# Parked scores fetched up to four blocks ahead, into the slots of the normed rows

## The chip, the cores and the metric

One core of one Trainium2 chip runs the whole program in one launch. The metric is the time of an execution on the device in microseconds, the median of several executions. SP below is SyncE, whose queue issues most of the DMAs.

## The reference

Two layers of a streaming encoder, for 512 prompt tokens (one new stream) and 128 sample tokens (8 running streams of 16), width 1024. Layer 0 mixes tokens by a gated convolution beside windowed attention, layer 1 by a gated linear recurrence (HGRN2). Each mixer is followed by PEER, a retrieval from 16,384 experts: product keys choose for every token and each of 8 heads the best 16 of them, and the output sums over the experts found

```python
for each token x, each head, each of its 16 experts e (index idx, gate g):
    y += g * gelu(dot(x, u[e])) * v[e]
```

Everything is float32; on TensorE a product of float32 is made of three products of high and low halves.

## The kernel before, in words

**Two ways through PEER.** The 128 sample tokens and the first 128 prompt tokens go the sparse way: POOL gathers the rows of u (line 880) and of v (line 913) by index, VectorE makes the dot products (line 884) and the weighted sums `yv` (line 920). The other 384 prompt tokens go the dense way, in `dense_peer`: all 16,384 experts in 128 blocks of 128. A block's scores are a product of the 384 normed rows `xhl` with 128 rows of u, and Gelu; they are multiplied by the gates of the block (`gch`, one table for four blocks, fetched at lines 1105 and 1107; the multiply is line 1110), split into halves `wt` (high on ScalarE, line 240, low on VectorE, line 241), and combined with the block's 512 KB of v (line 272, also split into `whi` and `wlo`) in 18 matmuls of 128 x 512, line 1122, that gather in six banks over all 128 blocks.

**Scores made ahead.** While the product keys are being chosen, TensorE has room. `ahead` makes the scores of the last blocks then and parks them in DRAM, `sd`, 192 KB a block: the last 72 of layer 0 (blocks 56 to 127), the last 94 of layer 1 (blocks 34 to 127). In the main loop `scores(k)` fetches such a block at line 1096; for the blocks before, it makes the product.

**Slots.** A name of a tile pool ("tag") has a fixed number of buffers; a tile takes the next, and the instruction that first writes it waits for the last use of the tile that had it. Fetched scores lie in "ge" (two slots); in layer 1, where `DEEP` is 126, in "ge" and "sq" by turns (four in all); in layer 0 `DEEP` is 54, so that the fetched blocks, 56 and up, have "ge" alone. A slot is free when the low half of the block that was in it has been taken (line 241). "xb" has four slots of 128 x 2 x 512. In the loop they hold four of the eight tiles of the normed rows `xhl`, which the last product reads (block 55 in layer 0, block 33 in layer 1). They have a second user in layer 0's loop: the sample tokens, which were done with PEER before, go on into layer 1's mixer while the prompt's loop runs. The sample's recurrence works in two units, and each unit takes two tiles of "xb" (`lins` in `hgrn`), one held until its outputs are made (`recur`, lines 669 to 715), the other until its states are (`states`, lines 717 to 735).

**Order.** Loop, sparse rows and recurrence are generators stepped by turns, and a list scheduler then orders each engine's instructions. In the loop `scores` runs one to two blocks ahead of `combine`. Each engine executes its instructions in this order, and a DMA issue that waits holds up SP's issues behind it.

Of the kernel before, what the change touches and what calls it, by code (L numbers as in the profile page):

```python
# [62 lines left out]
def kernel(ctx: ExitStack, tc: tile.TileContext, t: dict):  # L63
    nc = tc.nc
    V, S, P, T, Y = nc.vector, nc.scalar, nc.gpsimd, nc.tensor, nc.sync
# [10 lines left out]
    def tl(tag, shape, dt=F32, name=None):  # L76
        return sb.tile(shape, dt, name=name or tag, tag=tag, bufs=BUFS.get(tag, 1))
# [4 lines left out]
    def bank(tag):  # L82
        return ps.tile([128, 512], F32, name="p" + tag, tag=tag, bufs=1)
# [100 lines left out]
    def behind(ins, others):  # L184
        for d in others:
            tc.add_manual_dep(ins.ins, d.ins.name, mybir.DependencyInfo(
                mybir.DependencyClass.Sync, mybir.DependencyReason.DATA), reason="gates in DRAM")
# [33 lines left out]
    def small(tag, n, name=None):  # L221
        return tl(tag, [128, 512 if n > 128 or tag != "idf" else 128], name=name)[:, :n]
# [16 lines left out]
    def split(hi, lo, src):  # L239
        S.activation(hi, src, AF.Copy)  # L240
        return V.tensor_tensor(lo, src, hi.bitcast(F32), op=OP.subtract)  # L241
# [27 lines left out]
    def halves(tags, shape, src):  # L269

        raw = tl(tags[0], shape, name="wraw")
        Y.dma_start(raw, src)
        hi = tl(tags[1], shape, F32R, name="whi")
        lo = tl(tags[2], shape, F32R, name="wlo")
        d = split(hi, lo, raw)
        if tags[0] == "u4":
            mark[0] = d
        marks.append(d)
        return hi, lo

    def product2(p, w, xhl, first=None):
        for xv, wv in ((0, 0), (1, 0), (0, 1)):
            for k in range(8):
                m = T.matmul(p, w[wv][:, k], xhl(xv, k), start=(k == 0 and xv == wv), stop=(k == 7 and wv == 1))
                if first is not None:
                    follow(m, first)
                    first = None

    def product(p, w, xhl):
        for k in range(8):  # L290
            T.matmul(p, w[0][:, k], xhl(0, k), start=(k == 0), stop=False)  # L291
            T.matmul(p, w[0][:, k], xhl(1, k), start=False, stop=False)  # L292
            T.matmul(p, w[1][:, k], xhl(0, k), start=False, stop=(k == 7))  # L293
# [680 lines left out]
    def dense_peer(l, xhl, sv, si):  # L974

        G = GA
        n = G.n
        FIRST, EACH, NA = FE[l]
        AHEAD = list(range(128 - NA, 128))
        nt = len(G.tiles)  # L980
        gd = dr.tile([n // 32, 128, 128, 32], F32, name="gd", tag="gd", bufs=1)
        sd = dr.tile([len(AHEAD), 128, n], F32, name="sd", tag="sd", bufs=1)
# [106 lines left out]
        gch = {}  # L1089
        mult = [None, None]  # L1090

        def scores(k):
            deep = DEEP[l] > k
            ge = small(("ge", "sq")[k % 2] if deep else "ge", n)
            if k in AHEAD:
                Y.dma_start(ge, sd[AHEAD.index(k)])  # L1096
            else:
                w = halves(("u4", "uh", "lo"), [128, 8, 128], t["uT"][l, k])
                s = bank("b" if k < KB[l] and k % 2 else "s")[:, :n]
                product2(s, w, xhl, mult[1] if PEO[l] else None) if PO[l] else product(s, w, xhl)  # L1100
                S.activation(ge, s, AF.Gelu)
            if k % 4 == 0:
                gch[k // 4] = tl("g8", [128, n // 32, 4, 32], name="gch")
                if SC[l]:
                    behind(Y.dma_start(gch[k // 4][:, 0:4], gz[:, :, k:k + 4, :].rearrange("g p k t -> p g k t")), fences[-1:])
                g0 = 4 * SC[l]
                Y.dma_start(gch[k // 4][:, g0:], gd[g0:, :, k:k + 4, :].rearrange("g p k t -> p g k t"))
            g3 = ge.rearrange("p (g t) -> p g t", t=32)
            marks.append(None)
            marks[-1] = mult[0] = V.tensor_tensor(g3, g3, gch[k // 4][:, :, k % 4], op=OP.mult)  # L1110
            wt = tl(("w3", "nat")[k % 2] if deep else "w3", [128, 2, 384], F32R, name="wt")[:, :, :n]
            marks.append(split(wt[:, 0], wt[:, 1], ge))
            return wt
# [13 lines left out]
        for k in range(128):  # L1127
            while len(wts) <= (2 if DEEP[l] > k + 2 else 1):
                j = next(todo, None)
                if j is None:  # L1130
                    break
                wts[j] = scores(j)
                if DEEP[l] <= j + 1 and j not in vhs:
                    vhs[j] = values(j)
            for j in (k, k + 1):
                if j < 128 and j not in vhs:
                    vhs[j] = values(j)
            combine(k, wts.pop(k), vhs[k])
            mark[0] = mult[0]
            yield 1  # L1140
# [69 lines left out]
    for l in range(2):  # L1210
# [31 lines left out]
        xa = lambda v, k, xhl=xhl: xhl(v, k)[:, 128:512]  # L1242
        xt = lambda v, k, xhl=xhl: xhl(v, k)[:, 0:128]
        de = dense_peer(l, xa, sv[:, 1:4], si[:, 1:4])
        for i, _ in enumerate(route_p(l, xhl, sv, si)):
            if i < FE[l][0]:
# [124 lines left out]
```

## Time and profile before

| what | us |
|---|---|
| median of the runs | 4003.3 |
| range of the runs | 4000.8 to 4003.57 |
| the profiled execution's own time | 4001.81 |
| its span | 4000.1 |
| layer 0's loop, fetched blocks: from, to the last combine | about 1555, 2095.1 |
| of these, last weighted sum of layer 0's gathered rows | 1850.0 |
| sample's indices of layer 1 done (line 874) | 2162.0 |
| layer 1's mixer ends (line 339) | 2616.6 |
| layer 1's loop, fetched blocks: from, to the last combine | about 3540, 3969 |

Every time is of one core, and one profiled execution; the page divides the span into busy time by engine, slices, queues, the chain that ended last and groups of instructions. A group's busy time is not its cost: what counts is which engine the others wait for in that stretch. PE is TensorE, DVE VectorE, ACT ScalarE, POOL GpSimd; SPq is SP's queue of DMA issues.

### The profile page before, as it was taken

The page shows a single profiled execution, that of the slowest core. Times are in us where ns is not written, and L with a number is a line of the kernel's source. Part 1 is how long each engine was busy: PE and PEld are TensorE (multiplying, and loading weights), DVE is VectorE, ACT ScalarE, POOL GpSimd, SP SyncE. Part 2 cuts the span into 40 slices and gives each one's busy share as a digit, 9 for nine tenths or more (in the row PEclk, how much of TensorE's full clock was granted, in tenths as well). Part 3 has the DMA queues.
Part 4 walks back from the last instruction along what each step waited for, and adds up shares of the span by engine and source line. Part 5 has one row for each costly group of instructions (what it writes and reads, how often), then busy time and mean ns, then how long its engine had stood idle before and what let it go on. Part 6 is the DMA issues. An engine that isn't in the chain of part 4 may idle for free. (4 is left out here: it accounts for less than half of the span.)

```text
span 4000.1 us, 51433 instructions
## 1 busy us (share of the span) xinstructions
PE 3573.7 (89%) x17676; PEld 2922.7 (73%) x17676; DVE 3217.6 (80%) x6206; ACT 1654.5 (41%) x2717; POOL 1606.3 (40%) x1173
## 2 busy tenths in 40 slices
PE   6978788999999999788998777887999999999997
PEld 4756666789779998556776555566998988987775
DVE  5558999886568779988669877999998638888988
ACT  6544222467623334344434223331367733333332
POOL 0001665431235455541002544465078734454444
PEclk8989899999999999999999787798999999999998
DMA  4334998896689999999766775688467769999999
GB/s 143 118 105 155 333 341 312 314 344 246 248 301 338 338 340 349 376 347 316 238 204 227 268 237 201 214 319 309 138 170 200 200 202 349 339 361 388 385 385 328
DMA packets 491783, 1102.40 MB, mean 276 GB/s; under 512 B 55920, under 2 KB 271984, under 8 KB 486384
## 3 DMA queue, kind: packets, MB, share of 16 engines
q1 hardware_dynamic: 325632, 562.10, 40.4%
q0 software_dynamic: 165888, 537.01, 37.9%
q8 instruction: 139, 2.28, 0.2%
q14 instruction: 124, 1.02, 0.1%
HBM read 1008.28 MB, written 91.59 MB: 275 GB/s over the span
## 5 line engine op out<-in xcount | busy, mean ns | idle before, releaser
L240 ACT ACTIVATE whi<-wraw 128x1024 fp32r<-128x1024 f32 x710 | 741.5, 1054 | 1115.8 <-PE py L292 336.1
L241 DVE TENSOR_TENSOR wlo<-wraw,whi 128x1024 fp32r<-128x1024 f32 x710 | 861.6, 1216 | 339.5 <-ACT whi L240 174.3
L880 POOL DMA_INDIRECT gu<-u,idx x512 | 675.4, 1319 | 1059.2 <-DVE idx L874 425.6
L1122 PE MATMUL py<-whi,wt 128*128 128x512 f32 x3072 | 798.4, 405 | 53.7 <-ACT wt L240 48.0
L1122 PEld LDWEIGHTS py<-whi,wt 128*128 128x128 f32 x3072 | 581.7, 192 | 209.4 <-ACT wt L240 66.0
L913 POOL DMA_INDIRECT gv<-v,idx x384 | 510.0, 1328 | 530.7 <-DVE yv L920 355.7
L884 DVE CUSTOM_DVE_ANT_0 gu<-gu,xnn 128x1024 f32<-128x1024 f32 x512 | 614.8, 1217 | 59.0 <-DMA gu<-u,idx 58.4
L291 PE MATMUL py<-xhl,whi 128*128 128x512 f32 (+1 forms) x1392 | 540.2, 389 | 72.5 <-ACT xhl L240 30.5
L293 PE MATMUL py<-xhl,wlo 128*128 128x512 f32 (+1 forms) x1392 | 534.8, 385 | 24.5 <-DVE wlo L241 24.3
L292 PE MATMUL py<-xhl,whi 128*128 128x512 f32 (+1 forms) x1392 | 531.0, 381 | 10.7 <-DVE xhl L241 10.7
L920 DVE SCALAR_TENSOR_TENSOR yv<-gv,wact,yv 128x1024 f32<-128x1024 f32 x381 | 488.3, 1282 | 5.2 <-DMA gv<-v,idx 2.1
L291 PE MATMUL ps<-xhl,whi 128*128 128x384 f32 (+1 forms) x1168 | 403.4, 345 | 20.0 <-ACT whi L240 9.9
L293 PE MATMUL ps<-xhl,wlo 128*128 128x384 f32 (+1 forms) x1168 | 403.2, 345 | 6.0 <-DVE wlo L241 5.9
L1122 PE MATMUL py<-wlo,wt 128*128 128x512 f32 x1536 | 400.5, 393 | 0.7 <-DVE wlo L241 0.7
L292 PE MATMUL ps<-xhl,whi 128*128 128x384 f32 (+1 forms) x1168 | 399.8, 342 | 0.0
L291 PEld LDWEIGHTS py<-xhl,whi 128*128 128x128 f32 x1392 | 274.6, 197 | 131.6 <-ACT xhl L240 34.9
L1122 PEld LDWEIGHTS py<-wlo,wt 128*128 128x128 f32 x1536 | 288.0, 188 | 66.8 <-issue 1.2
L293 PEld LDWEIGHTS py<-xhl,wlo 128*128 128x128 f32 x1392 | 274.1, 197 | 83.3 <-DVE wlo L241 35.4
L1070 POOL DMA_INDIRECT gz<-gatea,ati x128 | 262.6, 2052 | 163.7 <-DVE mr L771 123.2
L292 PEld LDWEIGHTS py<-xhl,whi 128*128 128x128 f32 x1392 | 275.1, 198 | 47.2 <-DVE xhl L241 15.2
L944 POOL DMA_INDIRECT gv<-v,idt x128 | 155.3, 1213 | 318.9 <-PE pb L962 291.8
L291 PEld LDWEIGHTS ps<-xhl,whi 128*128 128x128 f32 x1168 | 222.4, 190 | 34.5 <-ACT whi L240 11.5
(444 smaller groups left out, 4859.7 us busy)
## 6 DMA issues: line engine op xcount, KB each, us to landing
wraw<-uT SPq DMA_DIRECT2D x256, 512.0 KB, 5.9
wraw<-v SPq DMA_DIRECT2D x256, 512.0 KB, 7.8
wraw<-w SPq DMA_DIRECT2D x98, 512.0 KB, 4.8
gd<-st SPq DMA_DIRECT2D x40, 1024.0 KB, 7.5
wraw<-wq SPq DMA_DIRECT2D x64, 512.0 KB, 5.9
sd<-ge SPq DMA_DIRECT2D x166, 192.0 KB, 3.7
gch<-gd SPq DMA_DIRECT2D x32, 768.0 KB, 9.3
ge<-sd SPq DMA_DIRECT2D x120, 192.0 KB, 9.3
```

The lines of the kernel that those rows point to most:

```text
L240: S.activation(hi, src, AF.Copy)
L241: return V.tensor_tensor(lo, src, hi.bitcast(F32), op=OP.subtract)
L291: T.matmul(p, w[0][:, k], xhl(0, k), start=(k == 0), stop=False)
L292: T.matmul(p, w[0][:, k], xhl(1, k), start=False, stop=False)
L293: T.matmul(p, w[1][:, k], xhl(0, k), start=False, stop=(k == 7))
L880: P.indirect_dma_start(out=rows[s], out_offset=None, in_=t["u"][l], in_offset=bass.IndirectOffsetOnAxis(ap=idx[:, s:s + 1], axis=0))
L884: d = V.tensor_tensor_reduce(out=g, in0=g, in1=xn, scale=1.0, scalar=0.0, op0=OP.mult, op1=OP.add, accum_out=w[:, s - LG:s - LG + 1])
L913: P.indirect_dma_start(out=rows[s], out_offset=None, in_=t["v"][l], in_offset=bass.IndirectOffsetOnAxis(ap=idx[:, s:s + 1], axis=0))
L920: d = V.scalar_tensor_tensor(y, rows[e], w[:, e:e + 1], y, op0=OP.mult, op1=OP.add)
L944: P.indirect_dma_start(out=rows[s], out_offset=None, in_=t["v"][l], in_offset=bass.IndirectOffsetOnAxis(ap=idt[:, tok[s]:tok[s] + 1], axis=0))
L1070: d = P.indirect_dma_start(out=flat, out_offset=bass.IndirectOffsetOnAxis(ap=ati[:, j:j + 1], axis=0), in_=gate[:, j:j + 1], in_offset=Non ...
L1122: mult[1] = T.matmul(yp[a][hf], wt[:, wv, 128 * a:128 * a + 128], vh[vv][:, 512 * hf:512 * hf + 512], start=(k == 0 and wv == 0 and vv == ...
```

## The change

`scores` no longer fetches its own block. A helper `fetch` keeps up to four blocks fetched, each in a tile of "xb", and `scores` takes its block from them; so a fetch is written in the program up to three blocks before the block's `scores`. The fetched scores leave "ge" and "sq" to the products. Nothing is added to the arithmetic, and no buffer is added.

```diff
--- before.py
+++ after.py
@@ -1089,12 +1089,24 @@
         gch = {}
         mult = [None, None]
 
+        fetched, todo_sd = {}, iter(AHEAD)
+
+        def fetch():
+
+            while len(fetched) < 4:
+                j = next(todo_sd, None)
+                if j is None:
+                    return
+                fetched[j] = tl("xb", [128, 512], name="sc")[:, :n]
+                Y.dma_start(fetched[j], sd[AHEAD.index(j)])
+
         def scores(k):
             deep = DEEP[l] > k
-            ge = small(("ge", "sq")[k % 2] if deep else "ge", n)
             if k in AHEAD:
-                Y.dma_start(ge, sd[AHEAD.index(k)])
+                fetch()
+                ge = fetched.pop(k)
             else:
+                ge = small(("ge", "sq")[k % 2] if deep else "ge", n)
                 w = halves(("u4", "uh", "lo"), [128, 8, 128], t["uT"][l, k])
                 s = bank("b" if k < KB[l] and k % 2 else "s")[:, :n]
                 product2(s, w, xhl, mult[1] if PEO[l] else None) if PO[l] else product(s, w, xhl)
```

In the changed kernel line 1101 is the fetch (1096 before), lines 1117 and 1119 fetch the gates (1105, 1107), and line 1122 is the multiply (1110; the combine is then line 1134). The scheduler orders layer 0's second half of the loop and layer 1's mixer anew. Three places:

SP, layer 0, the first fetches. `ge` or `sc` is a block's scores, `v0` the rows of v of layer 0, `w1` weights of the sample's recurrence, `st0` its states. Before:

```order
L272 DMA wraw_13198<-v0 128x1024
L272 DMA wraw_13132<-w1 128x4x256
L687 DMA s_in_13975<-st0 128x1024
L1096 DMA ge_12960<-sd_2968 128x384
L272 DMA wraw_13240<-v0 128x1024
L1107 DMA gch_13335<-gd_2967 128x12x128
L272 DMA wraw_13144<-w1 128x4x256
L1096 DMA ge_13004<-sd_2968 128x384
L272 DMA wraw_13341<-v0 128x1024
L272 DMA wraw_13383<-v0 128x1024
```

With the change:

```order
L272 DMA wraw_13138<-w1 128x4x256
L1101 DMA sc_12960<-sd_2968 128x384
L1101 DMA sc_12962<-sd_2968 128x384
L1101 DMA sc_12964<-sd_2968 128x384
L1101 DMA sc_12966<-sd_2968 128x384
L687 DMA s_in_13981<-st0 128x1024
L272 DMA wraw_13246<-v0 128x1024
L1119 DMA gch_13341<-gd_2967 128x12x128
L272 DMA wraw_13150<-w1 128x4x256
L272 DMA wraw_13347<-v0 128x1024
```

The first four fetches (blocks 56 to 59) now stand in a row, and each waits for the last product on TensorE; before, the first two stood four issues apart and waited for a "ge" slot.

VectorE, layer 0, around block 69 (`wlo` is a low half of v or of a weight, `yv` a weighted sum of gathered rows). Before, the row ahead of these is the low half of block 66, which frees the slot of block 68; the last row is block 68's multiply:

```order
L920 SCALAR_TENSOR_TENSOR yv_12254<-gv_13407,wact_9222,yv_12254 128x1024
L920 SCALAR_TENSOR_TENSOR yv_12254<-gv_13410,wact_9222,yv_12254 128x1024
L1110 TENSOR_TENSOR ge_13831<-ge_13831,gch_13614 128x384
L241 TENSOR_TENSOR wt_13834<-ge_13831,wt_13834 128x384
L241 TENSOR_TENSOR wlo_13941<-wraw_13938,whi_13940 128x1024
L920 SCALAR_TENSOR_TENSOR yv_12254<-gv_13413,wact_9222,yv_12254 128x1024
L241 TENSOR_TENSOR wlo_13559<-wraw_13556,whi_13558 128x1024
L920 SCALAR_TENSOR_TENSOR yv_12254<-gv_13416,wact_9222,yv_12254 128x1024
L241 TENSOR_TENSOR wlo_14035<-wraw_14032,whi_14034 128x1024
L241 TENSOR_TENSOR wlo_13571<-wraw_13568,whi_13570 128x1024
L920 SCALAR_TENSOR_TENSOR yv_12254<-gv_13501,wact_9222,yv_12254 128x1024
L1110 TENSOR_TENSOR ge_13930<-ge_13930,gch_13932 128x384
```

With the change, from the multiply of block 69 (`sc_13788`) to that of block 70 (`sc_13837`), whose slot block 69's low half `wt_14035` frees:

```order
L1122 TENSOR_TENSOR sc_13788<-sc_13788,gch_13938 128x384
L920 SCALAR_TENSOR_TENSOR yv_12254<-gv_13968,wact_9222,yv_12254 128x1024
L241 TENSOR_TENSOR wlo_13919<-wraw_13916,whi_13918 128x1024
L241 TENSOR_TENSOR wt_14035<-sc_13788,wt_14035 128x384
L920 SCALAR_TENSOR_TENSOR yv_12254<-gv_13971,wact_9222,yv_12254 128x1024
L241 TENSOR_TENSOR wlo_14078<-wraw_14075,whi_14077 128x1024
L920 SCALAR_TENSOR_TENSOR yv_12254<-gv_13974,wact_9222,yv_12254 128x1024
L920 SCALAR_TENSOR_TENSOR yv_12254<-gv_13977,wact_9222,yv_12254 128x1024
L1122 TENSOR_TENSOR sc_13837<-sc_13837,gch_13938 128x384
```

and SP's issues there:

```order
L272 DMA wraw_13880<-w1 128x4x256
L272 DMA wraw_13892<-w1 128x4x256
L272 DMA wraw_13904<-w1 128x4x256
L272 DMA wraw_13916<-w1 128x4x256
L1101 DMA sc_13788<-sd_2968 128x384
L272 DMA wraw_14075<-w1 128x4x256
L272 DMA wraw_14087<-w1 128x4x256
L1101 DMA sc_13837<-sd_2968 128x384
L272 DMA wraw_14099<-w1 128x4x256
L272 DMA wraw_14111<-w1 128x4x256
L272 DMA wraw_14476<-v0 128x1024
L1101 DMA sc_13936<-sd_2968 128x384
```

From block 69 on, each fetch takes the one slot that the block before has just left; block 69's own stands behind a run of loads of w1 and waits for the recurrence's matmuls of line 669. By the slots' addresses, one is left to the scores from block 69 to 75, two from 76 to 92, three to 113, four from 114 on: the rest belongs to the two units.

SP, layer 1, one period of four blocks. Before:

```order
L1105 DMA gch_29602<-gz_123 128x4x128
L1107 DMA gch_29602<-gd_20337 128x8x128
L272 DMA wraw_29609<-v1 128x1024
L1096 DMA ge_29600<-sd_20338 128x384
L1096 DMA sq_29561<-sd_20338 128x384
L272 DMA wraw_29648<-v1 128x1024
L272 DMA wraw_29687<-v1 128x1024
L1096 DMA sq_29642<-sd_20338 128x384
L1096 DMA ge_29681<-sd_20338 128x384
L272 DMA wraw_29726<-v1 128x1024
```

With the change:

```order
L1117 DMA gch_29608<-gz_123 128x4x128
L1119 DMA gch_29608<-gd_20337 128x8x128
L272 DMA wraw_29615<-v1 128x1024
L1101 DMA sc_29447<-sd_20338 128x384
L1101 DMA sc_29489<-sd_20338 128x384
L1101 DMA sc_29528<-sd_20338 128x384
L272 DMA wraw_29654<-v1 128x1024
L272 DMA wraw_29693<-v1 128x1024
L272 DMA wraw_29732<-v1 128x1024
L1101 DMA sc_29567<-sd_20338 128x384
```

Where a table of gates was followed by one row of v, two fetches, two rows, two fetches and a row, three fetches now stand behind the first row, then three rows and one fetch.

## Rows read from the trace of the kernel before

**Rows 1.** The page: busy time and share; the span in 40 slices.
```profile
PE 3573.7 (89%) x17676; PEld 2922.7 (73%) x17676; DVE 3217.6 (80%) x6206; ACT 1654.5 (41%) x2717; POOL 1606.3 (40%) x1173
...
DMA  4334998896689999999766775688467769999999
GB/s 143 118 105 155 333 341 312 314 344 246 248 301 338 338 340 349 376 347 316 238 204 227 268 237 201 214 319 309 138 170 200 200 202 349 339 361 388 385 385 328
```

**Rows 2.** Windows by stage: busy us, PEclk, DMA share, GB/s.
```profile
core 0: us, PE busy (x) PEld busy (x) DVE busy (x) ACT busy (x) POOL busy (x), PEclk, DMA share, GB/s
1555.00:1850.00 295.00, 238.09 (x993) 177.45 (x992) 260.72 (x296) 121.58 (x163) 141.83 (x100) 0.92 1.00 358
1850.00:2095.00 245.00, 232.98 (x1050) 179.67 (x1049) 168.12 (x352) 100.96 (x145) 0.00 (x0) 0.99 0.70 231
2095.00:2162.00 67.00, 51.06 (x222) 37.47 (x221) 62.30 (x168) 40.28 (x55) 0.09 (x1) 0.90 0.53 166
2162.00:2280.00 118.00, 99.52 (x459) 68.72 (x457) 103.43 (x207) 31.94 (x40) 71.03 (x59) 0.82 0.86 305
2280.00:2620.00 340.00, 274.53 (x1361) 186.34 (x1359) 280.26 (x515) 103.59 (x131) 155.12 (x118) 0.80 0.66 223
```

**Rows 3.** The fetch, line 1096, 1555 to 1850 us: who waited, landing.
```profile
L1096 SPq DMA_DIRECT2D ge<-sd x33: 320/336/3306, 1568.6 to 1842.5; - x33
...
  DVE ge L1110: 1.0, 1
...
DMA to landing us min/median/max: 4.0/8.1/13.6
```

**Rows 4.** The same for 1850 to 2100 us.
```profile
  DVE ge L1110: 36.9, 24
...
DMA to landing us min/median/max: 2.4/5.1/7.4
```

**Rows 5.** Timeline of TensorE, layer 1's loop: start, us, instructions, idle before.
```profile
3702.63 2.96 PE L1122 MATMUL py<-whi,wt 128*128 128x512 f32 x12
3705.43 1.54 PE L1122 MATMUL py<-wlo,wt 128*128 128x512 f32 x6
3706.80 2.95 PE L1122 MATMUL py<-whi,wt 128*128 128x512 f32 x12
...
3715.82 0.50 PE L1122 MATMUL py<-whi,wt 128*128 128x512 f32 x1 [0.53 <-ACT wt L240]
```

**Rows 6.** Timeline of SP's issues in the same stretch.
```profile
3697.68 0.37 SPq L1105 DMA_DIRECT2D gch<-gz  x1
...
3698.81 4.30 SPq L272 DMA_DIRECT2D wraw<-v  x1
...
3712.33 0.33 SPq L272 DMA_DIRECT2D wraw<-v  x1
3715.24 0.37 SPq L1105 DMA_DIRECT2D gch<-gz  x1
```

**Rows 7.** Timeline of VectorE in the same stretch.
```profile
3714.19 0.56 DVE L1110 TENSOR_TENSOR ge<-ge,gch 128x384 f32<-128x384 f32 x1 [1.68 <-DMA ge<-sd]
```

**Rows 8.** The chain that ended last, layer 1's loop: start, us, what.
```profile
3560.70 12.96 DMA sq<-sd
...
3598.14 10.74 DMA sq<-sd
```

**Rows 9.** Windows, layer 1's loop (columns as in rows 2).
```profile
3700.00:3800.00 100.00, 97.49 (x411) 77.75 (x411) 90.66 (x103) 34.50 (x45) 43.68 (x35) 0.98 1.05 385
```

**Rows 10.** Groups by line, VectorE, 1555 to 1850 us: busy, mean ns, idle.
```profile
L920 DVE SCALAR_TENSOR_TENSOR yv<-gv,wact,yv 128x1024 f32<-128x1024 f32 x105 | 134.3, 1279 | 0.7
L241 DVE TENSOR_TENSOR wlo<-wraw,whi 128x1024 fp32r<-128x1024 f32 x70 | 85.1, 1222 | 27.3 <-PE py L1122 12.5 <-ACT whi L240 12.5 <-issue 1.4
L1110 DVE TENSOR_TENSOR ge<-ge,gch 128x384 f32<-128x384 f32 x34 | 18.7, 551 | 1.0 <-DMA ge<-sd 1.0
L241 DVE TENSOR_TENSOR wt<-ge,wt 128x384 fp32r<-128x384 f32 x33 | 18.2, 551 | 1.5 <-ACT wt L240 1.5
```

**Rows 11.** Dot products, line 884, 2100 to 2700 us: what VectorE waited for.
```profile
  DMA gu<-u,idx: 41.7, 35
```

**Rows 12.** Waits of SP's queue, 3540 to 3970 us: total, times, longest.
```profile
SPq L1105 <- DVE sq L1110: 47.2, 22, 3.3
```

## Prediction

> **What bounds the kernel now.** I read the page's busy totals and slices first [rows 1]: TensorE is busy 89% of 4000.1 us, and the change works in two stretches only, the second halves of the two dense loops. Layer 0's fetched blocks run from about 1555 to 2095 us, layer 1's from about 3540 to 3970 us. The windows by stage [rows 2] then show that layer 0's stretch is two stages with different limits. Up to 1850 us the weighted sums of gathered rows run beside the loop: VectorE is busy 260.7 of 295 us and the DMA share is 1.00, while TensorE is idle for 57 us. From 1850 to 2095 us TensorE sets the pace (233 of 245 us), and VectorE is idle for 77 us. After the loop come the selection and the recurrence of the sample, bound in turn by VectorE and by gathers.
>
> Next I asked who waits for the fetch itself. In the first stage 33 fetches land 8.1 us after issue in the median (4.0 to 13.6), and VectorE waits for one of them, 1.0 us in all [rows 3]. In the second they land in 5.1 us and VectorE waits 36.9 us [rows 4], on an engine that has 77 us to spare. In layer 0 there is thus nearly nothing to win from an earlier fetch. In layer 1 TensorE takes 4.17 us for a block's eighteen matmuls (3702.63 to 3706.80) and waits 0.53 us before a pair of blocks [rows 5]; SP's table fetch comes back every 17.56 us, four blocks [rows 6], against 4 x 4.17 = 16.7 us of matmuls. VectorE's wait there is 1.68 us for a fetch [rows 7], and landings of 10.7 to 13 us lie on the chain that ended last [rows 8]. DMA stands at 385 GB/s and a share of 1.05 [rows 9].
>
> **What the change does.** It promises four slots. In layer 1 the scores already had four (two "ge", two "sq", used in turn), and now have four "xb": none is gained. In layer 0 they had two and get four, but only up to block 60: the sample's recurrence runs in this stretch and each of its two units takes two "xb" slots. From block 69 to 75 one slot is left to the scores, from 76 to 92 two as before, then three, then four. The order shows it: block 69's fetch stands behind a run of seven loads of w1, and only four VectorE rows lie between block 69's low half, which frees the slot, and block 70's multiply; with two slots there were eleven between such a release and its multiply.
>
> **Part by part, layer 0.** (1) Up to the last weighted sum, VectorE now does seven blocks fewer (the last sum falls near block 79, where it fell near 86) and four loads of the chain more. A block costs it a multiply (0.55), a low half of the scores (0.55) and one of the values (1.22) [rows 10], 2.32 us; 7 x 2.32 = 16.2 less, 4 x 1.22 = 4.9 more: **-11 us**.
>
> (2) With one slot, a fetch is issued only when the block before it has had its low half taken. I counted what VectorE has to do between that and the multiply, with the durations of [rows 10] (weighted sum 1.28, low half 1.22): 5.1 us for blocks 70 and 71, 8.7 for 72, 6.3 for 73 and 74, 11.4 for 75. Against a landing of 8.1 us the shortfalls are 3.0, 3.0, 0, 1.8, 1.8, 0, together 9.6; half a microsecond of issue for each of six makes **+13 us**. The bounds are 0, if all land near the fastest 4.0 us, and 6 x (13.6 - 5.1) = 51, if all take the longest. I take the median, since the same 512 KB rows and gathers run beside it. Before, with 12 to 17 us of cover, this was hidden; behind the waiting fetch stand loads of v, for which ScalarE's high half and TensorE wait.
>
> (3) The seven blocks go into the stage in which TensorE sets the pace: 7 x 4.17 = **+29 us**. The lower bound is 15, if half of that still fits into the 57 us in which TensorE idles before. In return the chain has fewer products left there (120 matmuls of line 312 behind block 79, 138 behind block 86 before, at 4.17/18 = 0.23 us, and some smaller ones): **-5 us**.
>
> (4) Part of the sample's selection, 35 us of VectorE's work, moves ahead of the loop's last multiply, where VectorE is idle. The indices come earlier and the gathers with them, for which VectorE waited 41.7 us [rows 11]. The work between the last multiply and the mixer's end shrinks by 15 us by the same count, and I add 3 us of the gather wait: **-18 us**; bounds 0 (the recurrence waits elsewhere) and -35.
>
> **Layer 1.** (5) The SP order changes from pairs (two fetches, two rows of v, two fetches) to three fetches, three rows, one fetch. VectorE's work between release and multiply stays (14.1 us before, 14.1 to 14.6 now), as do the bytes. The table of gates waits for one multiply fewer, half a microsecond; SP waited 47.2 us in all for it [rows 12]. 23 periods could give 23 x 0.5 = 11 us, but the DMA share is above 1 already [rows 9]; I take a third, **-4 us**. Bounds: -21 (below) and +5, if three fetches in a row delay the rows of v by as much as the gain.
>
> (6) The first four fetches wait for the last product on TensorE, since the normed rows hold their slots until then; before, the first needed only a "ge" slot. One landing of about 12 us [rows 8] less the 8.3 us that two queued blocks cover: **+4 us** (0 to 12). In layer 0 the same wait is covered by the products that VectorE and ScalarE still have in hand: 0.
>
> (7) Behind the last combine VectorE has three weighted sums fewer to do: 3 x 1.28 = **-4 us** (0 if the gathers, not the sums, end last).
>
> Sum: -11 + 13 + 29 - 5 - 18 - 4 + 4 - 4 = **+4 us**. The profiled execution took 4001.8 us, 1.5 below the median 4003.3, and would take 4006; on the scale of the median that is **4007 us**.
>
> **A rule against the trace.** The rows show 385 GB/s at a share of 1.05 [rows 9]; term 5 rests on that being nearly all there is. The Trainium skill (DMA: Bandwidth & Descriptors, "Where 436 GB/s comes from") says that transfers between HBM and SBUF are bound by the HBM side at about 358 GB/s, and gives 435 GB/s as the ceiling of the fabric. By 358 nothing could be won in layer 1, and the trace, which holds 385, disagrees with it as a bound; by 435 the estimate for a period would be 17.56 x 385/435 = 15.5 us, TensorE's 16.7 us would decide, and the loop would give the 21 us of the second rival.
>
> **Rivals.** *One slot queues everything behind it (slower).* SP issues in order. If the waiting fetch of blocks 70 to 76 pushes back the row of v behind it, the high half, its low half and the combine come late as well, and the next fetch with them. One issue of a row of v held SP for 4.30 us, others 0.33 [rows 6]; 7 x 4.3 = 30 us on top: **4037 us**. For it: this stage's DMA share is 1.00 [rows 2]. Against: the recurrence's work stands between and may fill TensorE. It decides if a row of v there is issued over 4 us after its buffer is free.
>
> *The fetch leaves the path (faster).* In layer 1 the landings on the chain [rows 8] were late by order, not by bytes. Three fetches at once, ahead of the rows of v, would let TensorE run at its own pace: 23.5 periods x (17.56 - 16.68) = 21 us in place of the 4 of term 5, so 4007 - 17 = **3990 us**. For it: TensorE's waits come before a pair of blocks and behind a fetch [rows 5, 7]. Against: a share of 1.05 leaves nothing to move the same bytes sooner. It decides if the table's period falls below 17.0 us.
>
> *The change does nothing that counts.* Layer 1 had four slots, and in layer 0 what is lost in one stage comes back in the next: 4000 to 4006 us; it lies inside my forecast's band.
>
> **How the numbers follow.** A measurement of this kernel can tell about 0.2% (8 us) from no change: 3995 to 4011 us is the same. My forecast, terms that nearly cancel, has 0.43 (own band 3994 to 4022: 0.25 same, 0.15 slower, 0.03 faster); the slower rival 0.27; the faster one 0.28; 0.02 are left for the unforeseen, on the same side as no change. That makes faster 0.31, same 0.27, slower 0.42. The range takes in both rivals with some of their bounds, the gain of term 4 doubled on one side and term 2 doubled on the other: 3974 to 4040 us.
>
> **What would show it.** Right: waits of VectorE for fetches in layer 0's first stage of 10 to 20 us, between blocks 69 and 75; the loop's last combine of layer 0 about 25 us later than at 2095 us; the sample's indices some 45 us behind that combine, where it is 67 now; layer 1's table every 17.3 to 17.6 us. Wrong: a fetch wait in that stage near zero (term 2), a loop of layer 0 that ends on time (term 3), a mixer that ends later by as much as the loop (term 4), or a period under 17 us in layer 1 (term 5).

## The result: slower by 1%, most of it in layer 0's loop and the stage behind it

The changed kernel takes **4043.1 us** in the median (4038.1 to 4047.7), against 4002.1 us for the kernel before on the same chip: a ratio of **1.0098 (1.0085 to 1.011)**. The profiled execution has a span of 4041.4 us, 41.3 more than that of before. The forecast was 4007 us, and its range ended at 4040.

Cutting both traces at the same instructions shows where the 41.3 us arise. The marks are the gate multiply of layer 0's block 54, the first add of the loop's output (line 1149, now 1161), the last add of layer 1's mixer (line 339), and the multiplies of layer 1's blocks 0, 32 and 127; each time is the start of that instruction in VectorE's timeline.

| stage | before, us | changed, us | difference |
|---|---|---|---|
| start to block 54 | 1563.9 | 1558.1 | -5.8 |
| layer 0's loop, block 54 to its end | 533.5 | 557.4 | **+24.0** |
| loop end to the mixer's end | 519.3 | 534.0 | **+14.7** |
| to layer 1's block 0 | 658.5 | 664.1 | +5.6 |
| layer 1, blocks 0 to 32 | 264.7 | 264.3 | -0.4 |
| layer 1, blocks 32 to 127 (fetched) | 421.3 | 425.0 | +3.7 |
| to the end | 39.0 | 38.4 | -0.5 |

The windows of the changed kernel, cut where its stages end (columns as in rows 2; to be held against rows 2):

```profile
1555.00:1850.00 295.00, 218.92 (x923) 161.69 (x922) 249.40 (x285) 115.62 (x158) 134.20 (x98) 0.84 0.95 340
1850.00:2112.00 262.00, 257.33 (x1125) 202.82 (x1124) 196.50 (x470) 108.11 (x152) 0.00 (x0) 1.00 0.68 226
2112.00:2179.00 67.00, 43.61 (x142) 28.51 (x141) 54.83 (x83) 29.42 (x42) 22.47 (x22) 0.77 0.94 309
2179.00:2297.00 118.00, 101.63 (x500) 70.27 (x498) 90.07 (x178) 39.27 (x47) 48.12 (x39) 0.92 0.69 226
2297.00:2650.00 353.00, 281.55 (x1362) 192.34 (x1361) 279.10 (x513) 103.43 (x131) 153.16 (x117) 0.79 0.65 212
```

Up to 1850 us TensorE was busy for 218.9 us, where it had been for 238.1 [rows 2]: 19 us of its work (70 matmuls) were left undone, in a stage where it had idled before. The next stage is TensorE's from end to end, 257.3 of 262 us, so what was left undone can only be added there: it has 75 matmuls and 24 us of TensorE's work more than before.

**The gap.** Where TensorE's work was lost is one place. Its timeline in the changed kernel, from the last matmuls of block 68 (line 1134 is the combine) to the first of block 69 (line 312 is a product of the sample's recurrence, line 669 its masked product):

```profile
1686.50 1.54 PE L1134 MATMUL py<-wlo,wt 128*128 128x512 f32 x6
...
1700.81 1.22 PE L312 MATMUL ps<-whi,xhl 128*128 128x512 f32 x2 [2.13 <-ACT whi L240]
...
1708.71 1.22 PE L312 MATMUL ps<-whi,xhl 128*128 128x512 f32 x2 [4.57 <-ACT whi L240]
...
1723.74 1.16 PE L669 MATMUL ps<-unit 128*128 128x128 f32 x8 [1.25 <-ACT fg L564]
1730.01 1.19 PE L312 MATMUL ps<-whi,xhl 128*128 128x512 f32 x2 [5.11 <-DVE at L671]
...
1742.34 1.98 PE L1134 MATMUL py<-whi,wt 128*128 128x512 f32 x6
```

For 54 us there is no combine; before, the longest such stretch from 1550 us to the loop's end was 9.5 us. What stands there is the recurrence's chain: load a weight, take its halves, multiply, wait for the next. SP's issues over the same time:

```profile
1692.86 40.85 SPq L272 DMA_DIRECT2D wraw<-w  x7
1733.80 0.46 SPq L1101 DMA_DIRECT2D sc<-sd  x1
```

The seven loads of w1, whose order stands in the section on the change, take 41 us to issue, since they wait for buffers that the chain frees and for earlier loads of w1 (SP waited 36.9 us for low halves and 20.1 us for such loads from 1684 to 1746 us), and block 69's fetch stands behind them. When SP came to it, the fetch did not wait for its slot at all: the matmuls of line 669 that free it ended at 1724.9 us, and the fetch left at 1733.8, right behind the seventh load. It was *placed* behind the chain, since its slot comes free only at line 669, so the order has everything up to there first. At block 72 the changed kernel is 61 us behind, at block 80 66 us; then, with the recurrence and the weighted sums done, it catches up to 18 us at the loop's end. A shorter stretch without a combine, 23 us from 1605.8 us on, costs nothing that is left: the look-ahead had put block 60 21 us early, and at block 68 the changed kernel is still 3 us early.

TensorE's clock fell with the gap as well. The window of before:

```profile
1650.00:1750.00 100.00, 78.09 (x304) 56.70 (x304) 84.91 (x88) 39.92 (x48) 46.00 (x36) 0.95 1.01 361
```

and of the changed kernel (PEclk is the first number behind POOL's: 0.95 before, 0.78 now):

```profile
1650.00:1750.00 100.00, 65.74 (x224) 46.79 (x223) 85.09 (x83) 38.50 (x45) 52.25 (x39) 0.78 0.96 345
```

**The fetch.** Who waited for it from 1555 to 1850 us, and its landing (rows 3 answer to these):

```profile
  DVE sc L1122: 7.7, 5
...
DMA to landing us min/median/max: 3.5/6.7/13.6
```

7.7 us in place of 1.0, of them 4.1 at blocks 65 and 66 and 3.6 at blocks 71, 72 and 74; from 1850 to 2112 us VectorE waits 36.0 us for it in 23 cases, as good as before [rows 4].

**Layer 1.** SP's issues, one period of the changed kernel (rows 6 answer):

```profile
3739.13 0.50 SPq L1119 DMA_DIRECT2D gch<-gd  x1
3740.54 5.87 SPq L272 DMA_DIRECT2D wraw<-v  x1
3746.50 2.36 SPq L1101 DMA_DIRECT2D sc<-sd  x3
3748.95 3.83 SPq L272 DMA_DIRECT2D wraw<-v  x3
3753.10 0.33 SPq L1101 DMA_DIRECT2D sc<-sd  x1
3757.53 0.38 SPq L1117 DMA_DIRECT2D gch<-gz  x1
```

The order is as built, three fetches and one, and the window from 3740 to 3840 us has the old rate (rows 9 answer):

```profile
3740.00:3840.00 100.00, 95.63 (x408) 75.62 (x407) 88.42 (x102) 34.41 (x44) 40.59 (x34) 1.00 1.05 385
```

385 GB/s at a share of 1.05, as in [rows 9]: the same bytes in the same time. A period of SP's table fetch is 17.8 us (20 periods from 3613.69 us on), where it was 17.6. The Trainium skill (DMA: Bandwidth & Descriptors, "Where 436 GB/s comes from") gives 435 GB/s as the fabric's ceiling and about 358 as what binds transfers between HBM and SBUF; the 385 held here, as before the change, lies above the second, and this window does not come to the first.

### The profile page after: what moved, and what is told of

The parts are those of the page before. It is cut to its first block, busy times and chain, and to the rows that moved or that the text cites. A ratio compares the mean times of both kernels' runs of the same rounds, so it can differ in the third digit from the quotient of the medians.

```text
span 4041.4 us, 51461 instructions
## 1 busy us (share of the span) xinstructions
PE 3586.9 (89%) x17676; PEld 2935.6 (73%) x17676; DVE 3218.9 (80%) x6206; ACT 1653.6 (41%) x2717; POOL 1589.8 (39%) x1173
## 4 chain that ended last, share of the span: by engine, by line
issue 15%; POOL 13%; DVE 9%; DMA 8%; PE 8%; ACT 1%; POOLq 0%; SPq 0%; DVEq 0%; ACTq 0%
POOL gz L1070 6%; DMA gu<-u,idx 4%; POOL gu L880 4%; POOL gv L913 3%; PE py L1134 2%; DVE wlo L241 2%; DMA gz<-gatea,ati 1%; DVE gu L884 1%; DMA wraw<-wq 1%; DVE yv L920 1%; PE py L291 1%; DMA sc<-sd 1%; PE py L292 1%; PE py L293 1%; DVE mr L771 1%
## 5 line engine op out<-in xcount | busy, mean ns | idle before, releaser
L913 POOL DMA_INDIRECT gv<-v,idx x384 | 499.1, 1300 | 548.6 <-DVE yv L920 357.8
L944 POOL DMA_INDIRECT gv<-v,idt x128 | 153.4, 1198 | 317.9 <-PE pb L962 291.5
```

The lines of the kernel that those rows point to most:

```text
L913: P.indirect_dma_start(out=rows[s], out_offset=None, in_=t["v"][l], in_offset=bass.IndirectOffsetOnAxis(ap=idx[:, s:s + 1], axis=0))
L944: P.indirect_dma_start(out=rows[s], out_offset=None, in_=t["v"][l], in_offset=bass.IndirectOffsetOnAxis(ap=idt[:, tok[s]:tok[s] + 1], axis=0))
```

## Experiments

Theories, with the letters used in the expectations. A: the loss comes from layer 0, where the recurrence's units take the slots. B: fetching several in a row crowds SP and DMA wherever it is done. C: what costs behind the loop is the order of the sample's key selection. F: dot products ahead of the mixer's first gate hold it up. G: a wait on POOL starves the first dot products. H: the gap is made good later, and the loop is long because the selection was drawn into it. Each run's stages, from its one profiled execution, as differences from the profile of before (us); "indices" is the time from loop end to the sample's indices (line 874):

| run | to block 54 | loop 0 | loop end to mixer end | to layer 1's block 0 | layer 1, blocks 32 to 127 | indices |
|---|---|---|---|---|---|---|
| before | 0 | 0 | 0 | 0 | 0 | 64.6 |
| changed | -5.8 | +24.0 | +14.7 | +5.6 | +3.7 | 13.5 |
| l1only | -0.5 | -3.1 | +3.3 | +0.4 | +1.3 | 64.7 |
| l0only | -2.0 | +26.2 | +11.6 | +5.7 | -0.7 | 13.5 |
| xb68 | -1.0 | -7.4 | +28.6 | +3.7 | +2.0 | 102.2 |
| xb93 | -3.4 | -1.8 | +21.0 | -0.3 | +3.9 | 97.6 |
| dep1 | -2.2 | +38.3 | +11.7 | +10.1 | -1.2 | 7.3 |
| x93pin | -4.6 | -3.0 | +7.5 | -5.4 | +1.7 | 63.5 |
| bpin | -1.4 | +3.5 | +0.6 | +6.2 | +0.1 | 64.8 |
| x68pin | +0.6 | +10.1 | +9.3 | +2.4 | +2.1 | 67.7 |
| bearly | -7.5 | +23.3 | +10.9 | +7.1 | -0.2 | 13.6 |
| alate | -5.2 | +25.7 | +13.3 | +5.8 | +0.4 | 27.4 |
| afg | -1.9 | +22.9 | +8.6 | +0.1 | -1.4 | 13.5 |
| astone | 0.0 | +25.7 | +1.9 | +2.9 | +2.0 | 13.5 |
| astone100 | -2.8 | +26.8 | +6.0 | +6.2 | +1.9 | 13.5 |
| aboth | -3.5 | +25.0 | +13.8 | +6.2 | -1.7 | 13.5 |
| bstone | +0.6 | +29.0 | +5.9 | +6.2 | +1.8 | 13.6 |

l1only and bpin leave layer 0's fetches as they were and still differ by 3 us here and there (bpin by 6 in one stage): differences of that size are not read below. A profile is one execution, and its time can lie some us off the median of its runs (bearly's 4036.6 us against a median of 4045.8, dep1's 4059.6 against 4052.5). The first column lies ahead of anything the edits touch and scatters by up to 7.5 us.

**Which layer.** The branch for fetched blocks is taken only where `l == 1` (or `l == 0`):

```diff
-            if k in AHEAD:
+            if k in AHEAD and l == 1:
                 fetch()
                 ge = fetched.pop(k)
+            elif k in AHEAD:
+                ge = small(("ge", "sq")[k % 2] if deep else "ge", n)
+                Y.dma_start(ge, sd[AHEAD.index(k)])
             else:
```

> Only layer 1 fetches ahead into the slots of the normed rows; layer 0 fetches as before. Theory A (the 41 us come from layer 0, where the sample's units take the slots): 4000 to 4012 us, layer 0's loop and mixer at the times of before, and a loop of layer 1 up to 6 us longer. Theory B (fetching three in a row crowds SP and the DMA queues wherever it is done): at least 15 us slower than before, in layer 1's loop.

4005.7 us, ratio 1.0011 (0.9993 to 1.003): no change that can be told.

> Only layer 0 fetches ahead into those slots. Theory A: 4030 to 4042 us, with the last combine of layer 0 some 17 us late and the end of layer 1's mixer some 33 us late, as in the changed kernel. Theory B: half of the loss, about 4020 us.

4039.5 us, 1.0092 (1.0066 to 1.0118). The whole loss comes with layer 0's fetches, as A has it; B falls.

**The slots, or looking ahead.** In xb68 layer 0 fetches ahead for blocks 56 to 68 only, in xb93 for 93 to 127 only (the condition above becomes `l or k < 69`, or `l or k > 92`, and the list of blocks to fetch is cut to match); dep1 uses the new slots without looking ahead:

```diff
-            while len(fetched) < 4:
+            while len(fetched) < 1:
```

> In layer 0 blocks 56 to 68 are fetched ahead into the slots of the normed rows, blocks 69 to 127 one by one into the two slots of before; layer 1 as changed. The stage with one slot is gone, and with it block 69's wait behind the recurrence. Theory A: no gap between the combines of blocks 68 and 69 of more than 15 us, layer 0's loop ends within 8 us of before, total 4000 to 4015 us. Theory B: the first thirteen blocks still cost, total above 4025 us.

4027.9 us, 1.0065 (1.0044 to 1.0086).

> In layer 0 blocks 56 to 92 are fetched as before, blocks 93 to 127 ahead into the slots of the normed rows, when three and then four of them are free; layer 1 as changed. Theory A: no loss in the gather stage, a loop end within 5 us of before, total 3998 to 4010 us. If look-ahead with free slots were worth something in the stage that TensorE paces, the loop would end at least 10 us earlier and the total be below 3995 us.

4022.7 us, 1.0054 (1.0033 to 1.0076). Neither total was expected by A (xb68's fits B's figure), but the place is not B's, and A's mechanism held: without the contest for slots the loop has no gap like that at block 69 and is not longer (-7.4 and -1.8 us). xb68 keeps the early stretch of 23 us without a combine, and its loop is the shortest of all, so that stretch is not what costs. The window of xb93 that the gap filled in the changed kernel:

```profile
1650.00:1750.00 100.00, 77.81 (x309) 56.39 (x309) 87.44 (x93) 41.73 (x51) 46.16 (x36) 0.96 1.03 376
```

TensorE 77.8 us, clock 0.96, as before. The 20 to 29 us were lost behind the loop, in a stage that the edits do not name: here the indices came some 35 us *later* than before.

> The scores go to the slots of the normed rows in both layers, but each block is fetched only where its scores are written, as before: the slots of the change without its look-ahead. Theory A (the slots are what costs): layer 0's loop has the gap where the recurrence takes its slots, total 4025 to 4045 us. Rival (the look-ahead costs): total within 8 us of before.

4052.5 us, 1.0123 (1.0106 to 1.0139): worse than the change, with the longest loop of all (+38.3 us), two gaps without a combine (1592 to 1620 and 1680 to 1728 us), and no look-ahead. The slots are what costs the loop, with or without looking ahead.

**The order of the selection.** In these the key selection of the sample, sixteen lists in four groups, is tied to the loop: an instruction-order edge without a semaphore, here for x93pin (bpin and x68pin have the same three edges on the kernel before and on xb68; bearly has `{100: 0, 107: 1, 116: 2, 123: 3}` on the kernel before; alate has the edge turned round, with `{111: 0, 118: 1, 125: 2, 127: 3}`, on the changed kernel):

```diff
             marks[-1] = mult[0] = V.tensor_tensor(g3, g3, gch[k // 4][:, :, k % 4], op=OP.mult)
...
+            if l == 0 and k in {114: 0, 121: 1, 127: 2}:
+                follow(mult[0], picks[1, {114: 0, 121: 1, 127: 2}[k]])
```

> As xb93 (layer 0 fetches ahead only from block 93 on), and the first three of the four groups of the sample's key selection are held ahead of the gate multiplies of blocks 114, 121 and 127, where they stood before. Theory C (xb93 lost its 20 us to a selection that came one group later, not to a fetch): the indices come within 8 us of before, the mixer of layer 1 ends at most 6 us late, total 3996 to 4008 us, and the loop's early end is gone as well. Rival: look-ahead with free slots is worth something by itself, the loop still ends 5 to 10 us early, total below 3996 us. If the 20 us were the fetch's, the total stays above 4015 us.

4000.1 us, 0.9996 (0.9987 to 1.0006). The 20 us of xb93 are gone with the order alone (13.5 of them in the stage behind the loop, 5.1 in the next); the loop's early end is mostly a start that was 4.6 us early. Look-ahead with free slots is worth nothing that can be measured.

> The kernel before with the three orders of x93pin and no fetch changed. If x93pin's earlier loop end (7.6 us) comes from the order alone, this loop ends 5 to 9 us earlier than before too and the total is within 4 us of x93pin's 4000 us. If it comes from the look-ahead with free slots, this loop ends within 3 us of before.

4006.7 us, 1.0011 (0.9993 to 1.0028); loop end 2.1 us late, as the expectation had it if the look-ahead is what gains. The loop itself is 6.5 us shorter in x93pin, little more than the scatter; the totals' difference, 6.6 us, lies in the profiles mostly in a stage that neither edit touches (-5.4 and +6.2 us). I read both as no change.

> As xb68 (blocks 56 to 68 of layer 0 fetched ahead, the others as before), with the selection held ahead of the multiplies of blocks 114, 121 and 127. Theory C: xb68's 26 us vanish, total 3994 to 4006 us, the best that look-ahead in layer 0 can give without the slots' contest; a gain of more than 8 us over before would show that look-ahead has a value after all.

4024.6 us, 1.0047 (1.0027 to 1.0068): a miss. The indices are back in place, but the loop is 10 us longer than before (17.5 longer than xb68's) and the stage behind it kept 9. So that xb68's loss is the selection's alone is not shown, and in this run a longer loop and a longer stage behind it come together without early indices.

> The kernel before, with no fetch changed; only the order is: the four groups of the sample's key selection are held ahead of the gate multiplies of blocks 100, 107, 116 and 123, so that the indices come as early as in the changed kernel. Theory C (the order of selection and dot products costs by itself): from loop end to mixer end 8 to 18 us longer than the 521 us of before, total 4006 to 4022 us. Rival (earlier indices help, as the prediction had it): 8 to 18 us shorter, total 3984 to 3996 us.

4045.8 us, 1.0109 (1.0092 to 1.0126): with no fetch changed, an early selection, held by hand, costs as much as the whole change. Behind the loop it is as C expected (+10.9 us); the total is not, since the loop has a gap of its own (+23.3 us; no combine from 1924.9 to 1968.2 us), where block 100's multiply stands behind the selection's chain. Before, TensorE was busy 46.5 and 49.5 us in these two windows, at a clock of 0.97 and 1.00; here:

```profile
1900.00:1950.00 50.00, 37.54 (x132) 25.71 (x131) 31.00 (x69) 17.74 (x31) 0.00 (x0) 0.85 0.62 211
1950.00:2000.00 50.00, 43.16 (x174) 32.19 (x173) 33.59 (x102) 16.84 (x22) 0.00 (x0) 0.87 0.62 199
```

That raised the question whether the changed kernel's loop is long for its gap or for the selection drawn into it.

> The changed kernel with the sample's key selection held back: its four groups stand behind the gate multiplies of blocks 111, 118, 125 and 127, about where they stood in the kernel before (in the changed kernel near 99, 106, 115 and 123). The gap at block 69 stays. Theory A (the slots' contest and its gap cost the loop): from block 54 to loop end still 550 us or more (before 533, changed 557), total 4020 to 4035 us. Theory H (the gap is made good later, and the loop is long because the selection was drawn into it): at most 543 us, and the total 4000 to 4018 us.

4042.2 us, 1.0095 (1.0071 to 1.0119). The loop is still 25.7 us longer with the selection held back: H falls, the gap costs the loop. The stage behind it did not recover (+13.3 us), though its indices came no earlier than 27 us behind the loop; the total, too, lies above what A expected.

**The stage behind the loop.** In the changed kernel POOL issues six gathers and then waits for the clearing of the gate table ("stone" is a mark that its stores wait behind):

```profile
2136.24 1.16 POOL L880 DMA_INDIRECT gu<-u,idx  x1 [0.30 <-issue]
2149.55 0.09 POOL L1063 MEMSET stone<- 1x1 f32 x1 [12.15 <-DMA gz<-zero]
2150.23 0.98 POOL L880 DMA_INDIRECT gu<-u,idx  x1 [0.59 <-DVE wact L884]
```

Before, the same mark came at 2120.6 us, 42 us ahead of the first gather. VectorE's wait for gathers in the changed kernel's stage (rows 11 answer):

```profile
  DMA gu<-u,idx: 72.7, 42
```

31 us more than in [rows 11]. Eight dot products stand ahead of the mixer's first forget gate there, where none did before. Two edges take the suspects apart:

```diff
+                if l and G is GS_ and s < 40 and 'fg' in hook:
+                    follow(d, hook['fg'])
...
+                if h == 0 and 'gu' in hook:
+                    follow(f, hook['gu'])
```

The first (afg) holds the sample's first dot products behind the mixer's first forget gate, the second (astone; `hook['gu']` is gather 40, in astone100 gather 100, counted from 0) the mark behind gathers. aboth has both; bstone has the second on bearly.

> The changed kernel with one order held: no dot product of the sample's gathered rows ahead of the first forget gate of layer 1's mixer (eight stood there). Theory F (VectorE's waits for gathers hold up the recurrence's start): the mixer ends 7 to 10 us earlier than in the changed kernel, total 4033 to 4037 us. Rival (the dot products bound the stage, wherever they stand): total 4040 to 4047 us.

4032.5 us, 1.0079 (1.0062 to 1.0095). The total fits F, the place less: the stage is 6 us shorter than in the changed kernel, the mixer ends only 3.3 us earlier; the other 8.9 us by which this profile is shorter lie behind the mixer.

> The changed kernel with one order held on POOL: the first store that waits for the clearing of the gate table stands behind 40 gathers of the sample, where it stood behind six. Theory G (that wait of 12 us starves the first dot products): from loop end to mixer end 5 to 12 us shorter than the 537 us of the changed kernel, total 4031 to 4038 us. Rival (the gathers are held by their buffers, not by that wait): no shorter than 534 us, total 4040 to 4047 us.

4032.4 us, 1.0075 (1.0051 to 1.0099); the stage is 521.1 us long, back to that of before within 2 us (the expectations counted this stage from the last combine, 2 to 3 us earlier than the table does).

> Both orders held, that of afg (no dot product ahead of the first forget gate) and that of astone. If the two waits together are what the early selection cost, loop end to mixer end comes back to 521 to 526 us and the total to 4020 to 4029 us; what is left then is the loop's 17 to 21 us. If the second does nothing, the total is that of afg, 4029 to 4036 us.

4040.5 us, 1.0087 (1.0055 to 1.012): the two do not add, and the stage is 13.8 us longer than before, though the mark is out of the way. POOL's timeline shows one wait put in the place of the other: with the dot products held, the seventh gather waits for one of them, 16.3 us where the mark's wait was 12.15.

```profile
2157.65 1.68 POOL L880 DMA_INDIRECT gu<-u,idx  x1 [16.30 <-DVE wact L886]
```

> As astone, with the store on POOL that waits for the clearing of the gate table behind 100 gathers of the sample in place of 40. Theory G (the wait of 12 us between gathers is what the early selection costs): from loop end to mixer end 519 to 527 us, as in astone (523), total 4026 to 4036 us. Rival (astone's shorter stage was chance, since aboth with the same order on POOL did not show it): 533 us or more, total 4038 us or more.

4039.6 us, 1.0078 (1.0058 to 1.0099); the stage is 525.3 us (+6.0; 528 counted from the last combine, at the edge of what G expected); the total is above it: the runs of the kernel before beside it had a median of 4007.3 us.

> As bearly (the kernel before with the selection held early and no fetch changed), with that store on POOL behind 40 gathers. Theory G: from loop end to mixer end at least 7 us shorter than bearly's 532 us, total 4026 to 4038 us, and the loop's 23 us stay. Rival: no shorter than 529 us, total 4038 to 4048 us.

4043.9 us, 1.0097 (1.0065 to 1.013); the stage is 5.0 us shorter than bearly's, less than G expected; counted as there it is 529.4 us, which fits the rival, and so does the total.

VectorE's waits for gathers do not decide it: 72.7 us in the changed kernel, 65.0 in astone, 66.1 in astone100, 66.8 in afg, 71.2 in aboth, 65.6 in bearly and 62.6 in bstone, against 41.7 before; bearly and astone wait alike, and their stages differ by 9 us. Where the mark alone is moved, the stage is 5 to 13 us shorter; with the first edge beside it, nothing is won. So POOL's wait is a part of the 15 us in three of four runs. It can't be all: in alate the mark stands ahead of the first gather (2142.3 and 2146.3 us), as before the change, and the stage is still 13.3 us longer. The rest stays open. No run is faster than the kernel before by more than the scatter.

## Why the prediction was wrong

**Term 4 failed, the stage behind the loop (-18 us, measured +14.7).** It is 33 of the 37 us between the sum forecast, +4, and the 41.3 measured. "The indices come earlier and the gathers with them" was right: 13.5 us behind the loop's end in place of 64.6, sooner still than forecast. That it would shorten the stage was not, and the mixer ends late by more than the loop, as the prediction had named for a sign against this term. The early gathers ran into POOL's mark; VectorE's dot products came to stand among the first steps of the mixer, where they waited 31 us more for gathers; and the selection's 35 us of work were gone from there (that it had filled this time is argued, not shown). My bound "0 (the recurrence waits elsewhere)" had left out that VectorE, too, executes in order. All five other runs with early indices (27.4 us behind the loop or less) and no mark moved have this stage 8.6 to 13.3 us longer, whether a fetch was changed (l0only, dep1, alate, afg) or not (bearly); with late indices it is 21 and 29 us longer (xb93, xb68). With the selection where it was and no order held, the stage is as before within 3.3 us (l1only); where it was put back by hand, it is 0.6 to 9.3 us longer (bpin, x93pin, x68pin). What the runs do not part: each of those with early indices has a longer loop as well, so a share of the stage's loss may belong to the longer loop. The early selection is shown to go with the loss, also without any fetch changed; by which waits, only in part.

**The loop's terms came out nearly right, but for where the time is lost.** Terms 1 to 3 give -11 + 13 + 29 - 5 = +26 us; measured +24.0, and 22.9 to 26.8 in six more runs with the same loop. Terms 1 and 2 together (+2) are the gather stage's length; its last sum came 2.2 us earlier, counted from block 54. Term 3 is the rest: from the last weighted sum to the loop's end 247 us before and 273.5 now, +26, against +24. The mechanism of term 3 held too: blocks that miss the first stage go into TensorE's, nine of them where I had counted seven (900 matmuls of the combine start behind the last sum, 734 before). Nine at 4.17 us would be +38; that +26 came of it is in part luck, since 48 other matmuls left this stage and TensorE idled 5 us of it in place of 12. And term 2 sought 13 us in six fetches of blocks 70 to 75 that land too late; VectorE waited 3.6 us for those. What puts the blocks back is the one gap ahead of block 69 (no such gap, no longer loop, in xb93 and xb68; the gap and the longer loop in l0only, dep1 and alate), which my own excerpt of SP's order showed (the run of w1 loads), and to which I gave no price.

**Layer 1 was right: nothing.** Terms 5 and 6 (-4 and +4) share the stage from block 32 on, which measured +3.7; term 7 (-4) measured -0.5; and l1only is no change as a whole. That the slots were four before and after, and that DMA was near its rate [rows 9], was the right reading; the gain of a part of a microsecond a period did not come (17.8 us against 17.6).

**The rivals.** The slower one gave 4037 us, near the 4043 measured, by another mechanism: it had rows of v held up behind a waiting fetch of blocks 70 to 76, and the fetch was itself behind the chain, once. The sign it named did not come: up to 1850 us SP's fetches waited for slots that line 241 frees 8.9 us in all, in five cases, the longest 3.9 us. The faster one needed a period below 17 us in layer 1; it was 17.8.

**No term at all** covered the start, 5.8 us early, which lies ahead of the edit and is luck, and the 5.6 us between the mixer's end and layer 1's first block. Nine profiles show 5.6 to 10.1 us there, bpin, which changes next to nothing, among them; three show 2.4 to 3.7, four none or a gain. As far as these runs go, the 5.6 us can't be put down to the change, and their cause stays open.

## What to carry to other kernels

A slot that a second user holds is not a slot: before moving a buffer, list who else takes it in the stretch where it is used, and what has to happen before each comes free. Under a list scheduler a wait for such a slot need not show up as a wait; here it showed up as another chain placed ahead, so look in the new order for the longest run of rows without the bounding engine's work and price that. And a stage behind the edit is only safe if its order is unchanged: here an order shift alone, held by hand (bearly), cost as much as the change itself.

## What the runs showed that I had not expected

Indices that came some 33 to 57 us earlier or later went with a next stage 11 to 29 us longer in every profile in which no other order of that stage was held by hand; in bearly, where the order alone was changed, it was 11. TensorE's granted clock, as a mean over stretches at 2.4 and at 1.2 GHz, fell where it had waited for the chain: 0.78 of full speed in the 100 us with the gap, 0.71 in alate's and 0.80 in dep1's, against 0.95 before. And the deeper fetch in layer 1 changed which wait ends last without changing the time: ScalarE waited 153.4 us for rows of v before and 32.3 now, and 141.4 us for multiplied scores now where it had waited 59.2.
